# A transformer block on one Trainium2 core: the shift's part of two bias sums as one-column TensorE products, and shorter chains of one-column operations

## The chip, the cores and the metric

The kernel runs on one core of a Trainium2 chip. The core has five engines that run at the same time, each through its own queue in order: TensorE multiplies (PE, and PEld for its weight loads), VectorE (DVE), ScalarE (ACT) and GpSimd (POOL) work elementwise, and SyncE (SP) issues the loads from memory. They wait for each other by semaphores. The metric is device time in microseconds. Before the change three runs took 2125.7, 2130.1 and 2131.35 us.

## The reference, cut to what matters

One layer on 512 positions of 2048 channels. A conditioning vector c gives six modulation vectors through w_ada; the first two, shift1 and scale1, modulate the normalized input, and one large projection w_in makes Fourier channels, queries, keys, values, gates and output gates of it.

```
mod = jax.nn.silu(c) @ w_ada + b_ada
shift1, scale1, gate1, shift2, scale2, gate2 = jnp.split(mod, N_MOD, axis=-1)
h = modulate(rms_norm(x, norm1_w), shift1, scale1)      # h * (1 + scale) + shift
p = h @ w_in
q_in, k_in, v_in = p[..., o1:o2], p[..., o2:o3], p[..., o3:o4]
```

Behind it come the Fourier mixer and four mLSTM heads, the output projection, and a gated feed-forward network with a depthwise convolution.

## The kernel before, in words

Channels lie on the 128 partitions, in 16 tiles (k = 0 to 15) of 128 channels x 512 positions. Every float32 operand of a product is split into a rounded high half and a low half (`split`, lines L120 on ScalarE and L121 on VectorE; tiles named wg0h, wg0l and so on), and a product is three: high by high, high by low, low by high (lines L235 to L237 in `kouter`).

The modulation vectors are made on VectorE: `ada_unit` loads 128 x 1024 numbers of w_ada (tile ad, names like ad0_7_0 for modulation 0, k = 7, half 0) and multiplies them by silu(c) with a sum along the row (L167), two units for each k. `ada_cols` then adds the two partial sums, the bias (and 1 for a scale) and, for a scale, multiplies by the norm's weight: two or three operations on a single column (L183, L186, L189). Eight ad buffers take turns.

The first stage ("o-gate", sums g0 to g7) runs over k with x times scale1's column A1, before shift and norm are known. While it runs, the sum of squares is collected.

The second stage (sums h0 to h5: queries and keys of three heads, 768 columns of weights a step, tiles wh0 to wh15, four raw buffers and three each of high and low halves) still multiplies the unshifted x. Meanwhile the shift's columns S1 are made, and `shift_tile` rebuilds every tile of the input as x times A1 times rb1 (the reciprocal root as a row, L456) plus S1: ht on VectorE (L433, L435, L436), then the high half mov on ScalarE (L439) and the low half on VectorE (L440). What shift contributes to the h sums has to be added as a bias for each output column. For the first head's query and key (256 columns) this is done from the raw weight tiles that are in memory anyway: qkb, a 128 x 256 tile, collects weight times S1 over k on VectorE (L442, L444), and at the end two products with a column of ones sum it over the partitions (L465). For all other columns the weights are read a second time (`bias_units`, tiles wb, accumulated into sb on VectorE). GpSimd multiplies the eight o tiles by rb1 once that is there. After the second stage come the first head's values with the gates (`natural_gates`, tiles v_0 to v_5), the fourth head's queries (q), and the heads.

All instructions are put in order by the framework, which plans each engine's queue from a simulated timeline of its own; only what is wrapped in `pinned` keeps the order of the source.

Of the kernel before, what the change touches and what calls it, by code (L numbers as in the profile page):

```python
# [10 lines left out]
F32 = mybir.dt.float32  # L11
# [3 lines left out]
ALU = mybir.AluOpType  # L15
PSUM = bass.MemoryType.PSUM

P = 128
D = 2048
S = 512  # L20
KT = D // P
# [30 lines left out]
def block_kernel(ctx: ExitStack, tc: tile.TileContext, xT, vec, wada, wg, wqk, wv0, wvu,  # L52
                 wout, wup, wdown, cst, rmask, ftab, crow, cvec, outT):
    nc = tc.nc
    mm = nc.tensor.matmul
# [17 lines left out]
    def T512(name, dt=F32):  # L73
        return tmp["p"].tile([P, S], dt, tag="t", name=name)
# [6 lines left out]
    def load_consts():  # L81
        nc.sync.dma_start(vt, vec)
        nc.scalar.activation(vcols("c", 0, KT), vcols("c", 0, KT), AF.Silu)
        ident0 = T512("ident0")
        nc.sync.dma_start(ident0[:, 0:P], cst[:, 0:P])
        nc.vector.tensor_copy(identr, ident0[:, 0:P])

    onesf = const.tile([P, P], F32, name="onesf")
# [14 lines left out]
    def vcols(n, i, w):  # L103
        return vt[:, VC[n] + i:VC[n] + i + w]

    def raw_tile(src, w, name):
        r = wp.tile([P, 1024], F32, tag="raw", bufs=4, name=name)
        nc.sync.dma_start(r[:, :w], src)
        return r
# [3 lines left out]
    def split(src, w, name, into=None):  # L113
        if into is None:
            hi = wp.tile([P, 1024], F32R, tag="whi", name=name + "h")
            lo = wp.tile([P, 1024], F32R, tag="wlo", name=name + "l")
        else:
            hi, lo = into[:, 0:1024], into[:, 1024:2048]
        put = tc.keep_in_program_order if inorder[0] else lambda i: i
        put(nc.scalar.activation(hi[:, :w], src, AF.Copy))  # L120
        put(nc.vector.tensor_tensor(lo[:, :w], src, hi[:, :w].bitcast(F32), op=ALU.subtract))  # L121
        return hi, lo
# [14 lines left out]
    def bcast_rows(ps, cols, put):  # L137

        dg = T512("dg")
        for j in range(cols.shape[1]):  # L140
            sl = slice(j * P, (j + 1) * P)
            nc.vector.tensor_scalar(dg[:, sl], ident, cols[:, j:j + 1], None, op0=ALU.mult)
            put(ps[:, sl], onesf, dg[:, sl], start=True, stop=True)
# [3 lines left out]
    adaD = const.tile([P, 2, KT, 4], F32, name="adaD")  # L147
# [10 lines left out]
    def ada_unit(mod, slot, k, u, w, sb, pool=None):  # L158

        if "ring" in ada:  # L160
            r = ada["ring"][k % 4]
        else:
            r = ada["p"].tile([P, w], F32, tag="ar", bufs=ada["n"], name=f"ad{mod}_{k}_{u}")
        nc.sync.dma_start(r, wada[mod, k, :, u * w:(u + 1) * w])
        part = adaD[:, slot, k, u:u + 1]
        if not ((k if w == S else u) % 2 if pool is None else pool):
            nc.vector.scalar_tensor_tensor(r, r, 1.0, sb, op0=ALU.mult, op1=ALU.mult, accum_out=part)  # L167
        else:
            ada["pool"] = nc.gpsimd.tensor_tensor(r, r, sb, op=ALU.mult)
            ada["late"].append((r, part))  # L170
            if w == S:
                ada_late(1 if "ring" in ada else 2)

    def ada_late(n):
        while len(ada["late"]) > n:
            r, part = ada["late"].pop(0)
            nc.scalar.activation(r, r, AF.Copy, accum_out=part)

    def ada_cols(dst, kind, mod, slot, k0, n, parts):

        ada_late(0)
        s = slice(k0, k0 + n)
        nc.vector.tensor_tensor(dst, adaD[:, slot, s, 0], adaD[:, slot, s, 1], op=ALU.add)  # L183
        for i in range(2, parts):
            nc.vector.tensor_tensor(dst, dst, adaD[:, slot, s, i], op=ALU.add)
        nc.vector.scalar_tensor_tensor(dst, dst, 0.0 if kind == "g" else 1.0, vcols("bada", mod * 16 + k0, n),  # L186
                                       op0=ALU.add, op1=ALU.add)
        if kind != "g":
            nc.vector.tensor_tensor(dst, dst, vcols(kind, k0, n), op=ALU.mult)  # L189
# [4 lines left out]
    def big_tiles(k):  # L194
        return mov512[:, k, :], mov512[:, KT + k, :]
# [4 lines left out]
    def side(name):  # L200
        return pss.tile([P, S], F32, tag="s", name=name)
# [3 lines left out]
    pst = pa.enter_context(ExitStack())  # L205
    pS = pst.enter_context(tc.tile_pool(name="pS", bufs=1))
    silb = pS.tile([P, D], F32, tag="silb", name="silb")
    ada.update(p=pS, n=8)
    o_t = [None] * 8

# [136 lines left out]
    def pinned(f, *a, **kw):  # L347
        return tc.keep_in_program_order(f(*a, **kw))
# [4 lines left out]
    def load_x(k):  # L353
        x = (pS if 8 <= k < 13 else pX).tile([P, S], F32, tag=f"x{k}", name=f"x{k}")
        pinned(nc.sync.dma_start, x, xT[k])
        x_t.append(x)
# [3 lines left out]
    def scale_tile(k):  # L360
        ak = A1[:, k:k + 1]
        for u in (range(2) if k else (1, 0)):
            ada_unit(1, 0, k, u, 1024, silb[:, u * 1024:(u + 1) * 1024], pool=False)
        if k == 0:
            load_x(0)
            load_consts()
        r = raw_tile(wg[k, :, 0:1024], 1024, f"wg{k}")
        if k + 1 < KT:
            load_x(k + 1)
        ada_cols(ak, "n1", 1, 0, k, 1, 2)  # L370
        t = x_t[k]
        bt[k], btl[k] = big_tiles(k)
        nc.scalar.activation(bt[k], t, AF.Copy, scale=ak)
        nc.vector.scalar_tensor_tensor(btl[k], t, ak, bt[k].bitcast(F32), op0=ALU.mult, op1=ALU.subtract)
        w = split(r, 1024, f"wg{k}")
        if k == 0:
            nc.scalar.activation(ssq1, t, AF.Square)
        else:
            sq = T512("sq")
            nc.scalar.activation(sq, t, AF.Square)  # L380
            nc.vector.tensor_tensor(ssq1, ssq1, sq, op=ALU.add)
        return w
# [9 lines left out]
    for k in range(KT):  # L392
        nxt = scale_tile(k + 1) if k + 1 < KT else None
        kouter(g_ps, *w, k)
        w = nxt
# [3 lines left out]
    def rstd_cols(ssqs, t, put=mm):  # L399

        cp = side("ssc")
        n = (t.stop - t.start) // P
        for j in range(n):
            for i, q in enumerate(ssqs):
                put(cp[:, j:j + 1], q[:, t.start + j * P:t.start + (j + 1) * P], onesf[:, 0:1], start=i == 0,
                    stop=i == len(ssqs) - 1)
        rc = tiny.tile([P, 4], F32, tag="rc", name="rc")[:, 0:n]
        rsqrt_cols(rc, cp[:, 0:n], n, 1.0 / D)
        return rc

    def row_rstd(rc, put=mm):

        rps = side("rps")
        bcast_rows(rps, rc, put)
        return rps[:, 0:rc.shape[1] * P]
# [11 lines left out]
    def shift_tile(k, r):  # L427

        sk = S1[:, k:k + 1]
        t = T512("ht")  # L430
        raw = 0 < k < 13
        if raw:
            nc.vector.scalar_tensor_tensor(t, x_t[k], A1[:, k:k + 1], rb1, op0=ALU.mult, op1=ALU.mult)  # L433
        else:
            nc.vector.tensor_tensor(t, bt[k].bitcast(F32), btl[k].bitcast(F32), op=ALU.add)  # L435
            nc.vector.tensor_tensor(t, t, rb1, op=ALU.mult)  # L436
        ada_cols(sk, "g", 0, 0, k, 1, 2)
        bt[k], btl[k] = big_tiles(k)
        nc.scalar.activation(bt[k], t, AF.Identity, bias=sk)  # L439
        nc.vector.scalar_tensor_tensor(btl[k], t, sk, bt[k].bitcast(F32), op0=ALU.add, op1=ALU.subtract)  # L440
        if k == 0:
            nc.vector.tensor_scalar(qkb, r[:, 0:256], sk, None, op0=ALU.mult)  # L442
        else:
            nc.vector.scalar_tensor_tensor(qkb, r[:, 0:256], sk, qkb, op0=ALU.mult, op1=ALU.add)  # L444

    w = g2_weights(0)
    rb1 = pX.tile([P, S], F32, tag="x0", name="rb1")
    rc1 = rstd_cols([ssq1], slice(0, S))
    qkb = pS.tile([P, 256], F32, tag="qkb", name="qkb")
    bias = const.tile([P, 14], F32, name="bias")  # L450
    done = []
    for k in range(KT):
        nxt = g2_weights(k + 1) if k + 1 < KT else None
        kouter(g_ps, *w[1], k)
        if k == 0:
            nc.vector.tensor_copy(rb1, row_rstd(rc1, partial(pinned, mm)))  # L456
        if k:
            shift_tile(*done.pop())
        shift_unit(k)
        done.append((k, w[0]))  # L460
        w = nxt
    shift_tile(*done.pop())
    cp = side("qkbp")
    for i in range(2):
        mm(cp[:, i:i + 1], qkb[:, i * P:(i + 1) * P], onesf[:, 0:1], start=True, stop=True)  # L465
    nc.vector.tensor_copy(bias[:, 8:10], cp[:, 0:2])
    raws = []
    for i, x in enumerate((7, 6, 2, 3, 4, 5)):
        r = pX.tile([P, S], F32, tag=f"x{x}", name=f"qkraw{i}")
# [217 lines left out]
    for h in range(NH):  # L687
# [9 lines left out]
        for i in range(2):  # L697
            j = 2 * h + i
            if j < 6:
                r = raws[j]  # L700
                nc.vector.tensor_scalar(r, r, bias[:, 8 + j:9 + j], None, op0=ALU.add)
            else:
                r = q3 if j == 6 else proj(1, "k3")
# [146 lines left out]
    for m in range(LAST[0]):  # L850
        if m < 4:
            ps = first[m][0]
        else:
            ps, g = wo_tile(m)
# [508 lines left out]
    for it, t in enumerate(TAIL):  # L1363
        n = t.stop - t.start
# [120 lines left out]
```

## Time and profile before

| | |
|---|---|
| median of three runs | 2130.1 us |
| profiled execution, its span | 2123.46 us, 2121.7 us |
| busy: TensorE, VectorE, ScalarE, GpSimd | 95%, 83%, 48%, 10% of the span |
| chain that ended last | TensorE 66%, DMA 15%, VectorE 13% |

The shares are averages over stages with different limits: the 16 accumulations (L442, L444) and the products L465 belong to the second stage alone, from 95 to 191 us of the span. How a stage runs is read from its own stretch: which engine never idles there, and what ends the idle time of the one that does. Engines work on instructions one behind another that overlap by a few hundredths of a microsecond, so the price of one is the distance from its start to the next start.

### The profile page before, as it was taken

The page shows a single profiled execution, that of the slowest core. Times are in us where ns is not written, and L with a number is a line of the kernel's source. Part 1 is how long each engine was busy: PE and PEld are TensorE (multiplying, and loading weights), DVE is VectorE, ACT ScalarE, POOL GpSimd, SP SyncE. Part 2 cuts the span into 40 slices and gives each one's busy share as a digit, 9 for nine tenths or more (in the row PEclk, how much of TensorE's full clock was granted, in tenths as well). Part 3 has the DMA queues.
Part 4 walks back from the last instruction along what each step waited for, and adds up shares of the span by engine and source line. Part 5 has one row for each costly group of instructions (what it writes and reads, how often), then busy time and mean ns, then how long its engine had stood idle before and what let it go on. Part 6 is the DMA issues. An engine that isn't in the chain of part 4 may idle for free.

```text
span 2121.7 us, 38452 instructions
## 1 busy us (share of the span) xinstructions
PE 2017.6 (95%) x15036; PEld 1931.7 (91%) x15036; DVE 1769.0 (83%) x2888; ACT 1020.3 (48%) x1469; POOL 221.6 (10%) x255
## 2 busy tenths in 40 slices
PE   8988998999899799999999999999999899999996
PEld 6877997998789699999999999999999899999996
DVE  8999978787777889899899999889888677777756
ACT  4422353443224655555555555555555455555553
POOL 0020000000000010101101101101100111111134
PEclk9999998999999899999999999999999999999998
DMA  9965846473887375676577577656667797887684
GB/s 373 367 232 189 288 140 199 159 247 130 302 282 260 85 215 157 194 216 191 162 222 222 156 211 213 183 179 200 196 161 292 244 288 212 246 246 196 161 237 153
DMA packets 165434, 456.41 MB, mean 215 GB/s; under 512 B 18354, under 2 KB 22978, under 8 KB 165252
## 3 DMA queue, kind: packets, MB, share of 16 engines
q1 hardware_dynamic: 135860, 371.64, 51.3%
q0 software_dynamic: 28304, 81.28, 17.9%
q8 instruction: 117, 1.92, 0.4%
q10 hardware_dynamic: 1088, 1.05, 0.1%
q14 instruction: 65, 0.53, 0.1%
HBM read 386.52 MB, written 67.37 MB: 214 GB/s over the span
## 4 chain that ended last, share of the span: by engine, by line
PE 66%; DMA 15%; DVE 13%; issue 3%; ACT 2%; POOL 1%; SPq 0%; POOLq 0%; DVEq 0%; ACTq 0%
DMA ad<-wada 4%; DVE ad L167 3%; DMA ring<-wada 2%; DMA gkept<-gh 2%; PE un L320 1%; PE un L318 1%; PE un L319 1%; PE g L235 1%; PE g L236 1%; PE g L237 1%; PE N L622 1%; PE wo L283 1%; PE wo L284 1%; PE wo L282 1%; PE vn L318 1%
## 5 line engine op out<-in xcount | busy, mean ns | idle before, releaser
L167 DVE SCALAR_TENSOR_TENSOR ad<-ad,silu 128x512 f32<-128x512 f32 x185 | 122.2, 686 | 17.8 <-DMA ad<-wada 17.4
L1326 POOL DMA_DIRECT2D xkept<-cr x80 | 68.8, 981 | 382.6 <-DVE cr L1131 364.3
L1193 ACT ACTIVATE u<-cr,cvt 128x512 f32<-128x512 f32 x88 | 71.6, 815 | 28.8 <-DVE cr L1129 27.3
L167 DVE SCALAR_TENSOR_TENSOR ad<-ad,silb 128x1024 f32<-128x1024 f32 x64 | 78.7, 1235 | 7.8 <-DMA ad<-wada 7.7
L1195 DVE SCALAR_TENSOR_TENSOR u<-cr,cvt,u 128x511 f32<-128x511 f32 x88 | 65.4, 745 | 0.5 <-ACT u L1193 0.5
L1196 DVE SCALAR_TENSOR_TENSOR u<-cr,cvt,u 128x511 f32<-128x511 f32 x88 | 65.5, 744 | 0.0
L167 DVE SCALAR_TENSOR_TENSOR ring<-ring,silu 128x512 f32<-128x512 f32 x71 | 47.2, 688 | 17.1 <-DMA ring<-wada 16.8
L1242 POOL DMA_DIRECT2D gkept<-gh x38 | 29.6, 779 | 235.9 <-ACT gh L1237 193.3
L1240 DVE TENSOR_TENSOR gst<-gst,gh 128x1024 fp32r<-128x1024 f32 (+1 forms) x38 | 41.4, 1089 | 11.6 <-ACT gh L1237 11.4
L1237 ACT ACTIVATE gh<-gst 128x1024 fp32r<-128x1024 f32 (+1 forms) x38 | 36.0, 947 | 29.0 <-DMA gkept<-gh 25.4
L1011 POOL DMA_DIRECT2D xkept<-xc x6 | 4.1, 681 | 422.1 <-DVE A L189 408.5
L283 PE MATMUL dz<-mov,dz_0h 128*128 128x256 f32 (+1 forms) x156 | 48.1, 309 | 0.0
L282 PE MATMUL dz<-mov,dz_0h 128*128 128x256 f32 (+1 forms) x156 | 47.9, 307 | 0.0
L284 PE MATMUL dz<-mov,dz_0l 128*128 128x256 f32 (+1 forms) x156 | 47.9, 308 | 0.0
L284 PE MATMUL wo<-mov,wo_8l 128*128 128x512 f32 x104 | 41.4, 398 | 3.6 <-DVE wo_8l L121 3.6
L282 PE MATMUL wo<-mov,wo_8h 128*128 128x512 f32 x104 | 40.8, 399 | 1.5 <-ACT mov L793 1.5
L283 PE MATMUL wo<-mov,wo_8h 128*128 128x512 f32 x104 | 41.3, 398 | 0.8 <-DVE mov L794 0.7
L284 PE MATMUL wo<-mov,wo_0l 128*128 128x512 f32 x104 | 40.7, 391 | 0.8 <-DVE wo_0l L121 0.8
L282 PE MATMUL wo<-mov,wo_0h 128*128 128x512 f32 x104 | 40.6, 391 | 0.0
L283 PE MATMUL wo<-mov,wo_0h 128*128 128x512 f32 x104 | 40.6, 390 | 0.0
L622 PE MATMUL N<-v,ph 128*128 128x258 f32 x160 | 35.0, 298 | 3.3 <-ACT hn L633 2.9
L120 ACT ACTIVATE dz_0h<-dz 128x768 fp32r<-128x768 f32 x26 | 22.0, 845 | 30.4 <-PE dz L283 23.6
(4032 smaller groups left out, 9411.0 us busy)
## 6 DMA issues: line engine op xcount, KB each, us to landing
ad<-wada SPq DMA_DIRECT2D x185, 256.0 KB, 4.6
ad<-wada SPq DMA_DIRECT2D x64, 512.0 KB, 8.6
mov<-gkept SPq DMA_DIRECT2D x52, 512.0 KB, 10.2
xkept<-cr POOLq DMA_DIRECT2D x80, 256.0 KB, 6.0
ring<-wada SPq DMA_DIRECT2D x71, 256.0 KB, 5.0
wo<-wout SPq DMA_DIRECT2D x32, 512.0 KB, 4.9
wb<-wg SPq DMA_DIRECT2D x48, 256.0 KB, 5.0
dz<-wdown SPq DMA_DIRECT2D x26, 384.0 KB, 3.5
```

The lines of the kernel that those rows point to most:

```text
L167: nc.vector.scalar_tensor_tensor(r, r, 1.0, sb, op0=ALU.mult, op1=ALU.mult, accum_out=part)
L282: mm(ps, wh[:, sl], rh[k], start=st, stop=False)
L283: mm(ps, wh[:, sl], rl[k], start=False, stop=False)
L284: mm(ps, wl[:, sl], rh[k], start=False, stop=sp)
L318: mm(acc[t], bt[k][:, sl], wh[:, sw], start=False, stop=False)
L622: mm(np_[:, 0:258], l[:, sl], v[:, r, t, :], start=i == 0, stop=i == n - 1)
L1193: nc.scalar.activation(u, r, AF.Identity, bias=cv(3, ch), scale=cv(1, ch))
L1195: nc.vector.scalar_tensor_tensor(u[:, 1:S], r[:, 0:S - 1], cv(0, ch), u[:, 1:S], op0=ALU.mult, op1=ALU.add)
L1196: nc.vector.scalar_tensor_tensor(u[:, 0:S - 1], r[:, 1:S], cv(2, ch), u[:, 0:S - 1], op0=ALU.mult, op1=ALU.add)
L1237: nc.scalar.activation(hi, part, AF.Copy)
L1240: nc.vector.tensor_tensor(lo, part, hi.bitcast(F32), op=ALU.subtract)
L1326: nc.gpsimd.dma_start(xkept[4 * d + 2 * j + r], rows[j][r], accum_op=ALU.add)
```

## The change

Two edits. In `ada_cols`, a single column with two partial sums is now made by one operation that adds both sums and the bias (a scale's bias plus 1 is made once for all 16 columns, b1p), followed for a scale by the multiplication with the norm's weight. And qkb is no longer a tile of VectorE: for each k two float32 TensorE products, with 128 raw weight columns as the stationary side and the column S1 as the moving side, add up in two PSUM columns qkb0 and qkb1, which are copied into the bias at the end.

```diff
     def ada_cols(dst, kind, mod, slot, k0, n, parts):
         ada_late(0)
+        if n == 1 and parts == 2:
+            col = [adaD[:, slot, k0, i:i + 1] for i in range(2)]
+            b = vcols("bada", mod * 16 + k0, 1) if kind == "g" else b1p[:, k0:k0 + 1]
+            nc.vector.scalar_tensor_tensor(dst, col[0], col[1], b, op0=ALU.add, op1=ALU.add)
+            if kind != "g":
+                nc.vector.tensor_tensor(dst, dst, vcols(kind, k0, n), op=ALU.mult)
+            return
...
+        if k == 0:
+            nc.vector.tensor_scalar(b1p, vcols("bada", 16, KT), 1.0, None, op0=ALU.add)
         ada_cols(ak, "n1", 1, 0, k, 1, 2)
...
-        if k == 0:
-            nc.vector.tensor_scalar(qkb, r[:, 0:256], sk, None, op0=ALU.mult)
-        else:
-            nc.vector.scalar_tensor_tensor(qkb, r[:, 0:256], sk, qkb, op0=ALU.mult, op1=ALU.add)
+        for i in range(2):
+            mm(qkb[i], r[:, i * P:(i + 1) * P], sk, start=k == 0, stop=k == KT - 1)
...
-    qkb = pS.tile([P, 256], F32, tag="qkb", name="qkb")
+    qkb = []
...
             nc.vector.tensor_copy(rb1, row_rstd(rc1, partial(pinned, mm)))
+            qkb += [side(f"qkb{i}")[:, 0:1] for i in range(2)]
...
-    cp = side("qkbp")
     for i in range(2):
-        mm(cp[:, i:i + 1], qkb[:, i * P:(i + 1) * P], onesf[:, 0:1], start=True, stop=True)
-    nc.vector.tensor_copy(bias[:, 8:10], cp[:, 0:2])
+        nc.vector.tensor_copy(bias[:, 8 + i:9 + i], qkb[i])
```

The planner orders the engines anew. TensorE in the second stage, where the products of the fourth weight tile (wh3) end: before, wh4 follows at once (h0 and h1 are sums, wh4h the high half).

```order
L237 MATMUL h5_881<-mov_76,wh3l_993 128x512
L235 MATMUL h0_876<-mov_76,wh4h_1029 128x512
L236 MATMUL h0_876<-mov_76,wh4h_1029 128x512
L235 MATMUL h1_877<-mov_76,wh4h_1029 128x512
L236 MATMUL h1_877<-mov_76,wh4h_1029 128x512
```

Now, at the same place (S1 is the shift's column, wh0 to wh4 without a letter the raw tiles):

```order
L245 MATMUL h5_867<-mov_76,wh3l_980 128x512
L452 MATMUL qkb0_931<-S1_84,wh2_939 128x1
L452 MATMUL qkb0_931<-S1_84,wh3_977 128x1
L452 MATMUL qkb1_932<-S1_84,wh0_868 128x1
L452 MATMUL qkb1_932<-S1_84,wh1_896 128x1
L452 MATMUL qkb1_932<-S1_84,wh2_939 128x1
L452 MATMUL qkb1_932<-S1_84,wh3_977 128x1
L452 MATMUL qkb0_931<-S1_84,wh4_1014 128x1
L452 MATMUL qkb1_932<-S1_84,wh4_1014 128x1
L243 MATMUL h0_862<-mov_76,wh4h_1016 128x512
```

The row broadcast of the reciprocal root and two more qkb products stand just ahead of these rows; before, that broadcast stood among the products of wh5. In the new order the qkb products of k = 5 to 7 stand between wh4h and wh4l, and those of k = 8 to 13 each behind the products of the next tile (k + 1).

ScalarE at the same time, from the high half of wh3 on. Before:

```order
L120 ACTIVATE wh3h_992<-wh3_990 128x768
L120 ACTIVATE wh4h_1029<-wh4_1027 128x768
L120 ACTIVATE wh5h_1066<-wh5_1064 128x768
L120 ACTIVATE wh6h_1103<-wh6_1101 128x768
L120 ACTIVATE wh7h_1140<-wh7_1138 128x768
L439 ACTIVATE mov_76<-ht_976,S1_84 128x512
```

Now:

```order
L120 ACTIVATE wh3h_979<-wh3_977 128x768
L449 ACTIVATE mov_76<-ht_963,S1_84 128x512
L449 ACTIVATE mov_76<-ht_1001,S1_84 128x512
L449 ACTIVATE mov_76<-ht_1038,S1_84 128x512
L449 ACTIVATE mov_76<-ht_1075,S1_84 128x512
L120 ACTIVATE wh4h_1016<-wh4_1014 128x768
L120 ACTIVATE wh5h_1053<-wh5_1051 128x768
```

Four high halves of shifted input tiles stand ahead of wh4h now. Also on ScalarE, earlier, wh1h stands behind the third copy of an o sum instead of ahead of the first.

VectorE around the low half wh4l. Before (rs_y, rs_z and rc belong to the reciprocal root, ad0_6_0 is the unit of k = 6):

```order
L167 SCALAR_TENSOR_TENSOR ad0_5_1_1135,adaD_89<-ad0_5_1_1135,silb_99 128x1024
L186 SCALAR_TENSOR_TENSOR S1_84<-S1_84,vt_77 128x1
L133 SCALAR_TENSOR_TENSOR rs_z_897<-rs_y_896 128x4
L183 TENSOR_TENSOR S1_84<-adaD_89 128x1
L444 SCALAR_TENSOR_TENSOR qkb_909<-wh4_1027,S1_84,qkb_909 128x256
L121 TENSOR_TENSOR wh4l_1030<-wh4_1027,wh4h_1029 128x768
L134 TENSOR_TENSOR rs_z_897<-rs_z_897,rs_v_895 128x4
L186 SCALAR_TENSOR_TENSOR S1_84<-S1_84,vt_77 128x1
L167 SCALAR_TENSOR_TENSOR ad0_6_0_1169,adaD_89<-ad0_6_0_1169,silb_99 128x1024
```

Now:

```order
L167 SCALAR_TENSOR_TENSOR ad0_10_1_1307,adaD_89<-ad0_10_1_1307,silb_99 128x1024
L443 SCALAR_TENSOR_TENSOR ht_1186<-x6_337,A1_83,rb1_874 128x512
L443 SCALAR_TENSOR_TENSOR ht_1223<-x7_382,A1_83,rb1_874 128x512
L167 SCALAR_TENSOR_TENSOR ad0_11_0_1341,adaD_89<-ad0_11_0_1341,silb_99 128x1024
L443 SCALAR_TENSOR_TENSOR ht_1260<-x8_427,A1_83,rb1_874 128x512
L443 SCALAR_TENSOR_TENSOR ht_1297<-x9_472,A1_83,rb1_874 128x512
L121 TENSOR_TENSOR wh4l_1017<-wh4_1014,wh4h_1016 128x768
L121 TENSOR_TENSOR wh5l_1054<-wh5_1051,wh5h_1053 128x768
```

The low half of wh4 stood between the ad units of k = 5 and k = 6; now it stands behind that of k = 11 and behind the ht of k = 9. On SyncE the load of wh4 moved from behind ad0_5_1 to behind ad0_11_0, followed there by those of wh5 to wh7, and the first twelve loads of the bias sums (wb) now stand among those of wh12 to wh15, ahead of the first value tiles.

## Rows read from the trace of the kernel before

**Rows 1.** Stretches (start:end us, length, busy us per engine, granted clock, DMA).
```profile
14.00:95.00 81.00, 81.00 (x348) 66.79 (x348) 80.02 (x158) 33.53 (x46) 0.00 (x0) 1.00 1.02 395
141.00:175.00 34.00, 20.39 (x73) 15.63 (x74) 34.00 (x63) 7.34 (x10) 0.34 (x1) 0.86 0.38 120
191.00:217.00 26.00, 24.91 (x197) 24.67 (x197) 22.85 (x41) 8.88 (x12) 0.00 (x0) 1.00 0.96 342
217.00:336.00 119.00, 119.00 (x878) 112.86 (x877) 100.55 (x233) 49.85 (x82) 2.15 (x1) 1.00 0.63 213
336.00:376.00 40.00, 31.24 (x207) 29.59 (x206) 32.30 (x113) 12.66 (x29) 0.00 (x0) 0.83 0.50 170
516.00:556.00 40.00, 32.61 (x160) 26.32 (x159) 34.98 (x96) 12.78 (x21) 0.00 (x0) 0.96 0.78 262
```

**Rows 2.** Timeline of PE, 104 to 192 us (start us, us, instruction, idle before).
```profile
104.39 0.94 PE L405 MATMUL ssc<-onesf,ssq 128*128 128x1 f32 x8
...
116.44 0.39 PE L235 MATMUL h<-mov,wh3h 128*128 128x512 f32 x1
...
120.52 0.39 PE L235 MATMUL h<-mov,wh4h 128*128 128x512 f32 x1
...
145.90 2.93 PE L237 MATMUL h<-mov,wh8l 128*128 128x512 f32 x6 [5.26 <-DVE wh8l L121]
...
152.04 0.42 PE L235 MATMUL h<-mov,wh9h 128*128 128x512 f32 x1
...
191.12 0.38 PE L341 MATMUL v<-v_0h,mov 128*128 128x272 f32 x1
```

**Rows 3.** Timeline of DVE, 98 to 162 us.
```profile
98.71 0.96 DVE L121 TENSOR_TENSOR wh1l<-wh,wh1h 128x768 fp32r<-128x768 f32 x1 [1.31 <-ACT wh1h L120]
...
105.37 0.16 DVE L130 TENSOR_SCALAR rs_v<-ssc 128x4 f32<-128x4 f32 x1 [2.03 <-PE ssc L405]
...
115.94 0.95 DVE L121 TENSOR_TENSOR wh4l<-wh,wh4h 128x768 fp32r<-128x768 f32 x1
...
126.41 0.68 DVE L456 COPY rb<-rps 128x512 f32<-128x512 f32 x1
...
155.73 1.22 DVE L167 SCALAR_TENSOR_TENSOR ad<-ad,silb 128x1024 f32<-128x1024 f32 x1
...
156.88 2.07 DVE L433 SCALAR_TENSOR_TENSOR ht<-x,A,rb 128x512 f32<-128x512 f32 x3
158.87 0.95 DVE L121 TENSOR_TENSOR wh10l<-wh,wh10h 128x768 fp32r<-128x768 f32 x1
...
161.54 0.48 DVE L444 SCALAR_TENSOR_TENSOR qkb<-wh,S,qkb 128x256 f32<-128x256 f32 x1
161.94 0.15 DVE L183 TENSOR_TENSOR S<-adaD 128x1 f32<-128x1 f32 x1
```

**Rows 4.** Timeline of ACT, 97 to 134 us.
```profile
97.83 0.85 ACT L120 ACTIVATE wh1h<-wh 128x768 fp32r<-128x768 f32 x1 [4.37 <-issue]
100.28 4.03 ACT L213 ACTIVATE o<-g 128x512 f32<-128x512 f32 x8 [1.60 <-PE g L237]
...
133.42 0.72 ACT L439 ACTIVATE mov<-ht,S 128x512 fp32r<-128x512 f32 x1 [8.00 <-DVE ht L436]
```

**Rows 5.** DMA issues, 0 to 240 us (KB each, median us to landing).
```profile
wh<-wg SPq DMA_DIRECT2D x16, 384.0 KB, 5.4
```

**Rows 6.** Timeline of DVE while GpSimd works, 127 to 142 us.
```profile
127.94 1.52 DVE L444 SCALAR_TENSOR_TENSOR qkb<-wh,S,qkb 128x256 f32<-128x256 f32 x1
129.38 2.31 DVE L167 SCALAR_TENSOR_TENSOR ad<-ad,silb 128x1024 f32<-128x1024 f32 x1
...
133.31 8.58 DVE L433 SCALAR_TENSOR_TENSOR ht<-x,A,rb 128x512 f32<-128x512 f32 x5
```

**Rows 7.** Timeline of POOL, 126 to 142 us.
```profile
127.24 14.09 POOL L348 TENSOR_TENSOR o<-o,rb 128x512 f32<-128x512 f32 x8 [126.80 <-DVE S L183]
```

**Rows 8.** Chain that ended last, 0 to 240 us (start us, us, work).
```profile
216.64 0.47 PE q L282
```

More of the change, by code (lines that the diff above doesn't have):

```diff
@@ L207, in block_kernel @@
     silb = pS.tile([P, D], F32, tag="silb", name="silb")
+    b1p = pS.tile([P, KT], F32, tag="b1p", name="b1p")
     ada.update(p=pS, n=8)
```

## The prediction

> **What bounds the kernel now.** I read the stretches first. From 14 to 95 us (the o-gate stage) TensorE never stops, 81.00 of 81.00 us, and VectorE is busy for 80.02. From 141 to 175, in the second stage (queries and keys of three heads, its sums called h), TensorE works for only 20.39 of 34 us, its granted clock averages 0.86, and VectorE is busy for all 34.00: there VectorE is the bound [rows 1]. TensorE's own rows name the place and the price. It stood 5.26 us for wh8l, the low half of the ninth weight tile, which VectorE writes; then six products took 2.93 us, and only at 152.04 were starts 0.23 apart again. The 14 products from 145.90 to 152.04 took 6.1 us where 14 of 0.227 (18 from 116.44 to 120.52) take 3.2: the stop cost another 3 us at the lower clock of 1.2 GHz [rows 2]. Last I read the order of the instructions of both kernels, since the change alters it on every engine up to the first tiles of the output projection and leaves it alone behind.
>
> **What goes and what comes.** VectorE loses 16 accumulations qkb at 0.40 us (start at 161.54, the next operation at 161.94 [rows 3]), 6.4 us, and 32 operations on one column at 0.07 to 0.15, some 3.5 us; it gains one 16-column operation and one more copy, 0.3 us. In the o-gate stage the saved columns buy nothing, as TensorE is the bound there. TensorE gains 32 one-column float32 products and loses two. The same form stands in the trace as ssc: four products of two passes each, 0.94 us, so 0.23 each and about 7 us in all [rows 2]. Where TensorE waits anyway they cost nothing. The two new PSUM tiles take the two side buffers that h4 and h5 leave; nothing else wants one before the stage ends.
>
> **What the order makes of it.** I walk the new order with the durations of the rows.
>
> *To 122 us.* In the o-gate stage nothing moves for TensorE, so h starts at 103.25 as before (five products ahead of ssc, 104.39 [rows 2]). ScalarE now has wh1h behind the third o copy instead of ahead of the first. The copies start at 100.28 and take 0.50 each, wh1h 0.85: done at 102.6 [rows 4]. VectorE stands at wh1l until then; before it went on at 98.71. With wh1l 0.9 (158.87) and two ad products of 1.15 (155.73 to 156.88) it begins the reciprocal root rs_v at 105.8, before at 105.37 [rows 3]: the wait has eaten what three accumulations and the columns saved. From rs_v to the copy rb1 it took 21.0 us before (126.41); of that two ad, three low halves, three accumulations and some columns, 6.4 us, no longer stand in front, which makes 120.4. TensorE gets there at about the same time: 71 products of 0.227, ssc and the row broadcast at some 0.85 each, 121.0 in all. rb1 is there at 121.7, some 5 us earlier than before.
>
> *The first new stop.* On TensorE eight qkb products follow (1.9 us, to about 123), and then those of wh4, ahead of wh4h. Two things hold them. The load of wh4 stood in SyncE's queue behind ad0_5_1; now it is behind ad0_11_0, which needs the buffer of ad0_7_0 (eight buffers, two a step), free at 120.9, and it also waits for the qkb product of k=0, at 122.1, because the raw tile is held until TensorE has read it. With 5.4 us to land [rows 5] it is there at 127.8. That is not the last: on ScalarE wh4h now stands behind four activations mov, and each of these waits for a tile ht of VectorE. In that stretch GpSimd multiplies the eight o tiles by rb1, and a VectorE operation then takes about 1.05 us more: qkb 1.52, ad 2.31, five ht 8.58 [rows 6], while GpSimd has its 14.09 us [rows 7]. From 121.7: ad 2.24, ht 1.7 and three ht 5.1 give 130.8, the fourth mov 0.7 [rows 4], wh4h 0.85: 132.3. TensorE stands from 123 to 132.3.
>
> At this place a rule bears on the sum. In these rows every VectorE operation with two tensors in SBUF pays the extra, and eight of them stand beside eight GpSimd operations. The Trainium skill ("SBUF — State Buffer", its terms, "shared port pair") says that the two engines lock one pair of ports for a whole instruction and the loser blocks; the trace agrees. By the price of the one slow accumulation its removal would give 1.44 us; by the rule the 14 us stay, another operation takes the place, and it gives 0.40. The walk above has the 14 us in either case.
>
> *The second.* TensorE does twelve wh4h products at the low clock (0.43 each, to 137.5) and the six qkb of wh5 to wh7, and then needs wh4l. VectorE had that at 115.94 [rows 3]; now it is behind the ht of k=9. From ad0_8_0, done at 136.4: six ad 6.9, eight operations on 512 columns at 0.66 (three from 156.88 to 158.87) 5.3, two columns 0.1, wh4l 0.9 [rows 3]: 149.6. TensorE stands from 139 to 149.6.
>
> *To the end of the stage.* From there TensorE has 204 products, 46.3 us, 3.0 for the low clock after the stop, and 20 qkb, 4.7: 203.6. The feed holds by my walk: wh7l at 158 against 162 needed, wh8l at 163 against 167; wh12 to wh15 load after the qkb product four tiles back and are split 1 to 3 us ahead of need. Before, the first product of the value stage started at 191.12 [rows 2]. So the stage ends 12.5 us later: 19.9 us of stops instead of 13.6, and 6 us of new products on the path.
>
> *Behind it.* The values took 24.91 busy of 26 us [rows 1] and VectorE has the same steps before q, so q starts about 12 us later than 216.64 [rows 8]. But the first loads of the bias sums no longer wait for the stage's last product: twelve are issued inside the stage, and nine more accumulations of 0.66 are done before q, 6 us of VectorE. TensorE cannot use that before 336, being busy for 119.00 of 119.00 from 217; from 336 to 376 it idles for 8.8 us at a clock of 0.83, from 516 to 556 for 7.4 [rows 1]. I let 3.5 come back, between none and 6. Sum: +12.5 − 3.5 = +9. The profiled execution took 2123.5 (span 2121.7); with +9 it is 2132.5. The median of the three runs lies 6.6 above it; I carry the difference: **2139 us**. Its own range: the walk may be off by 3 each way, and nothing or all 6 may come back: +3.5 to +15.5, 2134 to 2146.
>
> **Rivals.** *The relief reaches TensorE (faster).* TensorE stands 13.6 us for VectorE in 141 to 175 [rows 1], and VectorE has 9.6 us less to do. If all of it comes off those stops, and 10 of the 32 products lie outside them (2.3), the kernel gains 7.3: 2122.8. It turns on whether VectorE reaches wh4l before TensorE is through with wh4h; where it does, the second stop is gone. For it speaks the VectorE-bound stretch, against it the order, which puts wh4l behind a dozen long operations more. The far end would be all 13.6 us of stops and 3 of low clock gone, less 7 of products: −10.
>
> *The delay is absorbed (the same).* The idle 8.8 and 7.4 us after 336 are TensorE waiting while VectorE works through ad products. Their loads do not need h. If they keep their time, TensorE comes 12 later and finds them done: 9 or more come back, +3, 2133. Against it: in the new order these products still follow the bias sums in one queue.
>
> *The late loads miss (slower still).* wh13, wh14 and wh15 now stand behind bias loads in SyncE's queue, which wait for VectorE. My margins are 1 to 3 us; if three miss by 2 and the clock falls once (3), it is 9 more: 2148.
>
> **Chances.** The forecast 0.46, late loads 0.11, absorbed 0.26, faster 0.17. About 0.3%, 6.4 us, is what a measurement of this kernel can tell from no change. The forecast's lower edge lies inside that, the upper cases of the absorbed one outside, which nearly cancels: slower 0.56, the same 0.27, faster 0.17. The range leaves a tenth at either end, below the faster case and above late loads: 2122 to 2149.
>
> **What would show it.** Right: TensorE's waits name a qkb product or wh4h by ScalarE near 123 (9 us) and wh4l by VectorE near 139 (10 us); wh1l waits 4 us longer on VectorE; rb1 near 121; the stops for wh8l to wh12l are gone; the value stage starts near 203. Wrong: TensorE fed through wh4 and wh5, the value stage before 195, or a q that starts 12 late with the delay gone by 560.

## The result, and the profile after

The changed kernel takes 2142.4 us (median of 5 executions, 2139.6 to 2148.1) against 2130.1 (5 executions, the three above among them, 2123.1 to 2131.4): the ratio over all executions is 1.0072, 95% interval 1.0051 to 1.0092. It is slower by 12.3 us by the medians and by some 15 us by the ratio. The prediction was 2139 and slower. The profiled execution took 2139.63 us (span 2137.5, mean granted clock 0.977); that of before 2123.46 (2121.7, 0.983).

The stretches of the changed kernel, with the columns of [rows 1]. The first, fourth, sixth and last two answer to rows there; the other three lie ahead of the new stops, on the first of them, and behind.

```profile
14.00:95.00 81.00, 81.00 (x353) 66.93 (x352) 80.43 (x145) 34.14 (x45) 0.00 (x0) 1.00 1.03 403
95.00:120.00 25.00, 25.00 (x120) 20.98 (x119) 19.12 (x49) 6.32 (x11) 0.00 (x0) 1.00 0.67 226
120.00:141.00 21.00, 10.12 (x47) 8.70 (x45) 20.90 (x22) 5.09 (x7) 14.39 (x8) 0.64 0.65 230
141.00:175.00 34.00, 26.30 (x108) 21.65 (x109) 33.14 (x62) 8.25 (x11) 0.00 (x0) 0.82 0.50 164
175.00:203.00 28.00, 28.00 (x144) 23.75 (x144) 17.56 (x27) 8.95 (x12) 0.00 (x0) 1.00 0.54 176
203.00:229.00 26.00, 22.52 (x179) 22.29 (x177) 21.18 (x34) 6.89 (x10) 0.00 (x0) 0.99 0.89 301
348.00:388.00 40.00, 36.82 (x288) 35.56 (x288) 33.52 (x107) 13.54 (x30) 0.00 (x0) 1.00 0.57 183
528.00:568.00 40.00, 31.57 (x148) 25.53 (x147) 35.05 (x94) 11.13 (x18) 0.00 (x0) 0.91 0.85 295
```

VectorE had slack from 95 to 120 (19.12 of 25) and again from 175 on (17.56 of 28). In between it was full, and TensorE worked for 10.12 of 21 us at a clock of 0.64, and at 0.82 in the next stretch. So the relief did arrive on VectorE, but beside the stretch in which TensorE waits for it.

TensorE's timeline there, against [rows 2]:

```profile
102.81 0.95 PE L415 MATMUL ssc<-onesf,ssq 128*128 128x1 f32 x8
...
127.48 1.02 PE L452 MATMUL qkb<-S,wh 128*128 128x1 f32 x4 [5.37 <-DMA wh<-wg]
...
130.34 0.80 PE L243 MATMUL h<-mov,wh4h 128*128 128x512 f32 x1 [1.85 <-ACT wh4h L120]
...
148.70 2.93 PE L245 MATMUL h<-mov,wh4l 128*128 128x512 f32 x6 [11.37 <-DVE wh4l L121]
...
200.27 0.95 PE L452 MATMUL qkb<-S,wh 128*128 128x1 f32 x8
201.08 0.38 PE L349 MATMUL v<-v_0h,mov 128*128 128x272 f32 x1
```

Two stops stand in place of those for wh8l to wh12l: 5.4 and 1.9 us for wh4's load and its high half, then 11.4 us for its low half. The value stage starts at 201.08 instead of 191.12, 10.0 later. VectorE, against [rows 3, 6]:

```profile
101.50 0.96 DVE L121 TENSOR_TENSOR wh1l<-wh,wh1h 128x768 fp32r<-128x768 f32 x1 [5.77 <-ACT wh1h L120]
...
104.67 0.16 DVE L130 TENSOR_SCALAR rs_v<-ssc 128x4 f32<-128x4 f32 x1
...
120.22 0.69 DVE L464 COPY rb<-rps 128x512 f32<-128x512 f32 x1
...
121.97 1.75 DVE L446 TENSOR_TENSOR ht<-ht,rb 128x512 f32<-128x512 f32 x1
123.64 8.46 DVE L443 SCALAR_TENSOR_TENSOR ht<-x,A,rb 128x512 f32<-128x512 f32 x5
132.03 2.29 DVE L167 SCALAR_TENSOR_TENSOR ad<-ad,silb 128x1024 f32<-128x1024 f32 x1
...
134.25 1.22 DVE L185 SCALAR_TENSOR_TENSOR S<-adaD,vt 128x1 f32<-128x1 f32 x1
...
147.70 0.94 DVE L121 TENSOR_TENSOR wh4l<-wh,wh4h 128x768 fp32r<-128x768 f32 x1
```

rb1 is ready 6 us earlier than before. wh4l, which stood at 115.94, comes at 147.70, behind the ht and mov of the shift. ScalarE and SyncE's queue against [rows 4, 5], and GpSimd against [rows 7]:

```profile
100.61 0.86 ACT L120 ACTIVATE wh1h<-wh 128x768 fp32r<-128x768 f32 x1
...
128.83 0.72 ACT L449 ACTIVATE mov<-ht,S 128x512 fp32r<-128x512 f32 x1 [0.96 <-DVE ht L443]
129.46 0.83 ACT L120 ACTIVATE wh4h<-wh 128x768 fp32r<-128x768 f32 x1
```

```profile
121.50 2.02 SPq L108 DMA_DIRECT2D wh<-wg  x4
```

```profile
121.07 14.39 POOL L356 TENSOR_TENSOR o<-o,rb 128x512 f32<-128x512 f32 x8 [120.62 <-DVE rb L464]
```

Four loads of weight tiles leave right behind one another from 121.50, when the first products qkb have read the raw tiles.

Behind the value stage q starts at 230.6 instead of 216.64 [rows 8], 14.0 later, not 10. TensorE's wait there, and the accumulations sb of the bias sums on VectorE ahead of it:

```profile
PE q L290 <- DVE v L234: 5.1, 1, 5.1
```

```profile
173.95 0.49 DVE L505 TENSOR_SCALAR sb<-wb,S 128x512 f32<-128x512 f32 x1 [0.86 <-DMA wb<-wg]
...
185.75 0.75 DVE L510 SCALAR_TENSOR_TENSOR sb<-wb,S,sb 128x512 f32<-128x512 f32 x1
...
207.98 0.49 DVE L505 TENSOR_SCALAR sb<-wb,S 128x512 f32<-128x512 f32 x1
...
226.72 1.42 DVE L510 SCALAR_TENSOR_TENSOR sb<-wb,S,sb 128x512 f32<-128x512 f32 x2 [1.20 <-DMA wb<-wg]
228.06 0.17 DVE L672 COPY gt<-v 128x16 f32<-128x16 f32 x1
...
230.02 0.42 DVE L234 TENSOR_TENSOR v<-v,v 128x256 fp32r<-128x256 f32 x1
```

The copies gt and the splits of v stand behind 24 accumulations sb, each of which needs a load of its own; before, behind 14. Six of the 24 ran inside the second stage (173.95 to 186), the other 18 from 207.98 on in the value stage, where the 14 stood before. By the first product of the feed-forward part the delay is 6.8 us in this profile, and 9.8 in a second one (below).

### The profile page after: what moved, and what is told of

Its sections match the earlier page's. It is cut to its first block, busy times and chain, and to the rows that moved or that the text cites. A ratio compares the mean times of both kernels' runs of the same rounds, so it can differ in the third digit from the quotient of the medians.

```text
span 2137.5 us, 38499 instructions
## 1 busy us (share of the span) xinstructions
PE 2026.8 (95%) x15096; PEld 1943.9 (91%) x15096; DVE 1761.7 (82%) x2842; ACT 1018.3 (48%) x1469; POOL 220.5 (10%) x255
## 4 chain that ended last, share of the span: by engine, by line
PE 69%; DMA 13%; DVE 12%; issue 3%; ACT 2%; POOL 1%; SPq 0%; POOLq 0%; DVEq 0%; ACTq 0%
DMA ad<-wada 3%; DVE ad L167 2%; DMA ring<-wada 2%; DMA gkept<-gh 2%; PE un L326 1%; PE un L328 1%; PE un L327 1%; PE g L243 1%; PE g L244 1%; PE g L245 1%; PE N L629 1%; PE vn L328 1%; PE vn L327 1%; PE vn L326 1%; PE wo L292 1%
## 5 line engine op out<-in xcount | busy, mean ns | idle before, releaser
L1247 DVE TENSOR_TENSOR gst<-gst,gh 128x1024 fp32r<-128x1024 f32 (+1 forms) x38 | 41.4, 1089 | 12.4 <-ACT gh L1244 12.4
L510 DVE SCALAR_TENSOR_TENSOR sb<-wb,S,sb 128x512 f32<-128x512 f32 x44 | 31.5, 744 | 5.8 <-DMA wb<-wg 5.7
```

Source lines behind the costliest of these rows:

```text
L1247: nc.vector.tensor_tensor(lo, part, hi.bitcast(F32), op=ALU.subtract)
```

## The experiments

All of them ran beside the kernel before. The table gives what the later points use: how much later than in before's first profile the value stage (v), q, and the feed-forward's first product (up) start, the length of the stretch from that product to the last product of the down stage, and the ratio of the times with its interval. The starts were read to 0.1 us, so a difference can be 0.1 off.

| kernel | v | q | up | stretch, us | ratio |
|---|---|---|---|---|---|
| before (first profile) | 191.1 | 216.6 | 690.7 | 1410.5 | |
| before2 | +0.2 | −0.4 | +0.7 | 1422.1 | 1.0013 (0.9999–1.0027) |
| after (first profile) | +10.0 | +14.0 | +6.8 | 1418.9 | 1.0072 (1.0051–1.0092) |
| after2 | +10.0 | +14.6 | +9.8 | 1419.3 | 1.0070 (1.0056–1.0084) |
| cols | +2.6 | +4.1 | +0.4 | 1421.7 | 1.0007 (0.9991–1.0023) |
| qkb | +12.4 | +18.1 | +10.2 | 1420.8 | 1.0051 (1.0034–1.0068) |
| none | −6.3 | −3.9 | −5.6 | 1419.0 | 0.9968 (0.9954–0.9983) |
| hold | +7.5 | +10.5 | +8.5 | 1412.0 | 1.0035 (1.0022–1.0049) |
| half | +6.7 | +6.9 | +0.3 | 1414.9 | 1.0003 (0.9990–1.0016) |
| inord | +6.3 | +7.1 | −0.1 | 1418.5 | 1.0000 (0.9986–1.0015) |
| late | −2.9 | −0.9 | −1.9 | 1422.4 | 0.9989 (0.9970–1.0009) |
| late2 | −2.6 | −0.7 | −3.3 | 1425.1 | 0.9994 (0.9979–1.0008) |
| pool | −3.3 | −1.3 | −4.0 | 1416.5 | 0.9979 (0.9963–0.9996) |
| poolin | −4.9 | −0.3 | −2.5 | 1426.8 | 0.9998 (0.9981–1.0016) |

**cols: the fused columns alone.** The kernel before with the new branch of `ada_cols` and `b1p`; the sums stay as they were.

> The kernel before with the fused column operations alone; the sums stay on VectorE. Theory A (the one-column products hold the raw tiles and two PSUM banks, the order built around that hold puts the splits of wh4 to wh7 behind the shift work, and TensorE stops twice): the order of these splits stays that of before, no 11 us stop for wh4l; 2127 to 2132 us, ratio to before 0.999 to 1.001. Rival B (the fused columns, by the shorter VectorE chain, moved the splits): the 11 us stop for wh4l is here too, and 2137 to 2143 us.

No difference in time that can be told. TensorE's two longest waits from 95 to 240 us are those of before (4.8 and 5.3 us there), for low halves of later tiles; none is for wh4l:

```profile
PE h L245 <- DVE wh12l L121: 5.5, 1, 5.5
PE h L245 <- DVE wh8l L121: 4.6, 1, 4.6
```

Rival B falls: the fused columns do not bring the stop for wh4l, and the 2.6 us at v and 4.1 at q by which this kernel is later are gone by up (0.4).

**qkb: the products alone.** The changed kernel without the branch and `b1p`.

> The kernel before with the sums as one-column products alone; the columns are computed as before. Theory A (hold and order): both stops of TensorE, for wh4h near 130 us and for wh4l near 148 us, 2138 to 2146 us, ratio 1.004 to 1.008. Rival B (the fused columns moved the splits): wh4l waits under 3 us, 2130 to 2135 us, the price of the 32 products being about 4.7 us.

2139.4 us. Both stops are here, and the wait at q; the last row is one more wait:

```profile
PE h L237 <- DVE wh4l L121: 10.8, 1, 10.8
PE q L282 <- DVE v L226: 6.8, 1, 6.8
PE qkb L442 <- DMA wh<-wg: 6.1, 1, 6.1
PE qkb L442 <- DVE rb L454: 1.1, 1, 1.1
```

So the loss belongs to the sums' part of the change. The last row names what the products wait for at their start: the copy rb1. Of the four side tiles in PSUM, h4 and h5 hold two, and the row broadcast holds one until rb1 is copied from it; so the products of the second column, and with them the raw tiles, wait for rb1.

**none: neither products nor accumulations.**

```diff
-        for i in range(2):
-            mm(qkb[i], r[:, i * P:(i + 1) * P], sk, start=k == 0, stop=k == KT - 1)
...
-        nc.vector.tensor_copy(bias[:, 8 + i:9 + i], qkb[i])
+    nc.vector.memset(bias[:, 8:10], 0.0)
```

> The changed kernel without the first head's shift sums (the two bias columns are set to zero; nothing else is left out): VectorE is relieved of the sixteen operations and TensorE has no product in their place. Theory A (hold and order): the splits of wh4 to wh6 stand ahead of the four mov again, no stop over 4 us for a split between 120 and 150 us, the value stage begins near 184 to 188 us (7 to 3 us ahead of before), 2118 to 2126 us. Rival C (the products' own time on TensorE is the loss): the time is that of the changed kernel less 5 us, 2136 to 2139 us. Rival D (the relief of VectorE is worth nothing): 2129 to 2132 us.

2122.3 us, 6.8 below before by the ratio: the relief of VectorE is worth that much. The loads of wh3 to wh7 leave one at a time as the splits free their tiles, the first and last of five being

```profile
102.31 0.33 SPq L108 DMA_DIRECT2D wh<-wg  x1
...
118.01 0.33 SPq L108 DMA_DIRECT2D wh<-wg  x1
```

wh4l is split early, and no stop of TensorE between 120 and 150 us is over 2.6 us:

```profile
113.87 0.95 DVE L121 TENSOR_TENSOR wh4l<-wh,wh4h 128x768 fp32r<-128x768 f32 x1
```

```profile
133.20 1.65 PE L245 MATMUL h<-mov,wh6l 128*128 128x512 f32 x6 [2.07 <-DVE wh6l L121]
140.18 1.66 PE L245 MATMUL h<-mov,wh7l 128*128 128x512 f32 x6 [2.60 <-DVE wh7l L121]
```

Rivals C (2136 to 2139) and D (2129 to 2132) both fall.

**hold: the hold without the products.** To `none` one ScalarE operation on one column is added in `shift_tile`:

```diff
+        hold = tiny.tile([P, 1], F32, tag="hold", name="hold")
+        nc.scalar.activation(hold, r[:, 0:1], AF.Identity, bias=bt[k][:, 0:1].bitcast(F32))
```

> The kernel without the sums (they are left out, two bias columns zero), with one more ScalarE operation of one column per block that reads the raw tile and the shifted tile, and so holds each raw tile until its shift is in; no product is added on TensorE. The order of the splits then is that of the changed kernel. Theory A (the hold and the order that follows from it): the stops of the changed kernel come back, wh4l's at 9 to 13 us, though TensorE has no product more; the value stage at 194 to 198 us against 184.8 without the hold; 2127 to 2135 us. Rival C (the products on TensorE make the loss): as the kernel without the sums, 2119 to 2125 us.

2134.9 us. TensorE has nothing more to do than in `none`, and the stops are back, 24.1 us in all instead of 18.6 in the changed kernel:

```profile
131.11 0.79 PE L243 MATMUL h<-mov,wh4h 128*128 128x512 f32 x1 [10.29 <-ACT wh4h L120]
...
150.37 2.08 PE L245 MATMUL h<-mov,wh4l 128*128 128x512 f32 x4 [13.78 <-DVE wh4l L121]
```

with the four loads together again (the queue, then VectorE):

```profile
126.82 4.15 SPq L108 DMA_DIRECT2D wh<-wg  x4
```

```profile
149.38 0.94 DVE L121 TENSOR_TENSOR wh4l<-wh,wh4h 128x768 fp32r<-128x768 f32 x1
```

This settles what makes the stops. The stop for wh4l (13.8 us) and the start of v (198.6) lie just beyond what theory A expected, the time inside it. Holding the raw tile until the shift is in, and the order of splits that follows, costs 0.67% of the time against `none`, some 14 us, and 13.8 us at v, without one product on TensorE.

**half: one product per tile.** The loop over `i` in `shift_tile` runs once, and there is one PSUM column instead of two; the key sums are left out.

> The changed kernel with one of the two products of each tile (the key sums' product is left out, and the query sums stand in both bias columns): half of the products' work on TensorE, the same hold of the raw tiles and of a PSUM bank behind rb1, and the same order of the splits. Theory A (hold and order): both stops as in the changed kernel, wh4l's at 10 to 12 us; the changed kernel less the half of 5 us: 2138 to 2142 us. Rival C (the products' own time, or what it does to TensorE, is the loss): half of the distance to the kernel without the sums comes back, 2130 to 2134 us.

2130.5 us: theory A missed by 8 to 12 us, and the number is rival C's. The stops are there all the same:

```profile
127.71 0.58 PE L452 MATMUL qkb<-S,wh 128*128 128x1 f32 x2 [5.44 <-DMA wh<-wg]
131.40 0.79 PE L243 MATMUL h<-mov,wh4h 128*128 128x512 f32 x1 [3.10 <-ACT wh4h L120]
147.29 2.93 PE L245 MATMUL h<-mov,wh4l 128*128 128x512 f32 x6 [10.32 <-DVE wh4l L121]
```

At v it is 3.3 us ahead of the changed kernel: the second stop ends 1.4 us earlier (147.29 instead of 148.70), and eight products fewer behind it are the other 1.9. The next 4 come at q: here 16 accumulations sb of the value stage stand ahead of the first copy gt instead of 18, and q waits 1.3 us instead of 5.1. So up to q this is the products' price and the order once more, not a new cost of a product. Up to the feed-forward part the distance is 6.5 us, 9.5 from the second profile; the times are 12 (medians) to 15 (ratios) apart. The rest is not settled. Nor do the stops alone make the loss over before: `half` has 18.9 us of them, as many as the changed kernel, and the time of before. It makes up 6.6 us between q and up, where `hold`, 0.8 us later at v, makes up 2.0; what decides that no run shows.

**inord: products and hold as they are, the splits' order fixed.** `inorder[0] = True` from the stage's first split to its last, so that `split` keeps the order of the program on ScalarE and VectorE.

> The changed kernel with the splits of the second stage held in the order of the program on ScalarE and VectorE: wh3l and wh4l then stand between the shift work instead of behind it, and wh4h behind three mov instead of four. The hold of the raw tiles stays. Theory A in the form that the order of the splits on VectorE is most of the loss: the stop of 11 us for wh4l falls under 5 us, others of 1 to 3 us stay, 2128 to 2136 us. Theory A in the form that the hold of the raw tiles alone sets it (wh4 lands late whatever the order): 2139 to 2146 us.

2131.2 us, the time of before: with the splits' order fixed the whole loss is gone, and the hold is still there. The stop for wh4l is gone. Two are left, 12.6 us instead of 18.6, now for wh3, and longer than the 1 to 3 us expected:

```profile
126.54 0.80 PE L243 MATMUL h<-mov,wh3h 128*128 128x512 f32 x1 [5.63 <-ACT wh3h L120]
...
139.58 2.92 PE L245 MATMUL h<-mov,wh3l 128*128 128x512 f32 x6 [6.94 <-DVE wh3l L121]
```

v is 3.7 us ahead of the changed kernel, and q 6.9, with a wait of 1.8 us there; the rest of the 15 us comes back behind q, as in `half`.

**late and late2: products without a hold.** They stand behind the loop and read the 256 columns from loads of their own. In `late` these loads fetch columns 0 to 255, not those that the sums are over; `late2` fetches the right ones.

```diff
+    for j in range(4):
+        q = pS.tile([P, 1024], F32, tag="ar", bufs=8, name=f"qw{j}")
+        nc.sync.dma_start(q.rearrange("p (k c) -> p k c", k=4),
+                          wg[4 * j:4 * j + 4, :, 1024:1280].rearrange("k p c -> p k c"))
...
+            mm(cp[:, i:i + 1], qw[k // 4][:, o:o + P], S1[:, k:k + 1], start=k == 0, stop=k == KT - 1)
```

> The changed kernel with the 32 products moved behind the loop: they read the 256 columns from four loads of their own (2 MB more DMA) into tiles that the shift's modulation blocks leave, so no raw tile is held for them; columns fused. Theory A (hold and order): no stop over 4 us between 120 and 150 us; the time of the kernel without the sums plus 32 products at two passes of 0.09 us, 5 us or less: 2121 to 2131 us. Rival C (the products' own time on TensorE is the loss): as the changed kernel, 2138 to 2144 us. Rival E (the extra 2 MB of loads delay the weights of the stage that follows): the value stage starts with a wait on a load, 2132 to 2140 us.

> As the kernel with the products behind the loop, but its four loads read the columns 1024 to 1279 of the weights that the sums are over (the one before read columns 0 to 255, the same amount). The same order, so the same time: 2124 to 2133 us, ratio to before 0.997 to 1.001. If where the columns lie in memory mattered, it would differ from it by over 5 us.

2129.4 and 2126.2 us; the two agree. No stop in the second stage is over 2.6 us. The 64 passes of `late2` on TensorE:

```profile
171.91 1.39 PE L478 MATMUL qkbp<-S,qw 128*128 128x1 f32 x12
177.33 1.62 PE L478 MATMUL qkbp<-S,qw 128*128 128x1 f32 x14
184.38 4.30 PE L478 MATMUL qkbp<-S,qw 128*128 128x1 f32 x38
```

They are 7.3 us of busy time, and v comes 3.8 us later than in `none`. About half of it does not show there, because `none` waits 4.4 us ahead of v for VectorE (qkraw, the h sums times rb1), and the run of 38 stands in that place. The times are 4 to 6 us above `none` by the ratios, which uses up what the relief brings. Neither rival C nor rival E is seen.

**pool: the sums on ScalarE and GpSimd.**

```diff
+        d = r[:, 0:256] if k else qkb
+        nc.scalar.activation(d, r[:, 0:256], AF.Copy, scale=sk)
+        if k:
+            nc.gpsimd.tensor_tensor(qkb, qkb, d, op=ALU.add)
```

> The sums neither on VectorE nor on TensorE: ScalarE scales the 256 columns of each raw tile by the shift's column (in place, behind the split), GpSimd adds them up; the column is computed right behind its modulation block; columns fused. GpSimd's products with rb1 move behind these sums. Theory A (the loss is the hold and the order, the relief of VectorE is worth about 7 us): the order of the splits is nearly that of the kernel without the sums, no stop over 5 us, 2120 to 2127 us. Rival F (GpSimd's additions slow VectorE's operations with two inputs beside them, or the scaling delays the splits on ScalarE): 2129 to 2138 us.

2123.2 us, 4.5 below before by the ratio and 0.9% below the changed kernel: the fastest version that computes everything, though the gain over before is small beside what can be told. GpSimd's additions take 1.28 us on average (19.2 for 15, 0.77 to 2.02 each) and the longest stop for a split is 4.3 us:

```profile
151.92 0.79 PE L245 MATMUL h<-mov,wh9l 128*128 128x512 f32 x1 [4.30 <-DVE wh9l L121]
```

**poolin: the same with the splits in the order of the program.**

> The kernel with the sums on ScalarE and GpSimd, with the splits of the second stage in the order of the program besides. If the waits of 1 to 4 us for splits that it still has are the order's doing, 2116 to 2122 us; if they are VectorE's load, 2121 to 2127 us; if the fixed order makes ScalarE and VectorE wait at the head (wh0 behind the scaling), 2128 to 2136 us.

2126.0 us, ratio 0.9998: no gain on `pool`, nor a clear loss. v is 1.6 us earlier, but q waits 5.7 us. The waits for splits stay (2.8, 3.9 and 2.6 us are the longest), so the order does not make them, and TensorE waits only 0.9 us for wh0 at the head. The time lies in the range for VectorE's load, but that this load makes the waits is not shown apart. The fixed order helped where it took the place of a bad one.

**after2 and before2: both kernels again.**

> The changed kernel unaltered, with more executions. If the part of its loss that appears in the feed-forward stage of its profile (7 us over before's profile, with the same instructions in the same order) is the scatter of single executions: 2136 to 2142 us and a ratio to before of 1.004 to 1.006. If it is the change's: ratio 1.006 to 1.008.

> The kernel before unaltered, with another profile. If before's first profile was a short one of a scatter: the stretch from the first product of the feed-forward's first block to the last product of the down stage takes 1414 to 1425 us here, as in the other kernels, against 1410.5 in the first; the time 2126 to 2133 us, ratio 1.000. If it is a property of this kernel: 1409 to 1412 us again.

The changed kernel takes 2142.7 us (2140.3 to 2145.2), and the ratio of 1.0070 is in the range of the second reading: with more executions the loss does not shrink. Before's second profile has the same v, q and up within 0.7 us, and a stretch behind of 1422.1 us against 1410.5: it varies by 12 us between two executions of one kernel, and the changed kernel's 1418.9 and 1419.3 lie between. So the 8 us by which the first profiles differ there can't be put down to the change, and profiles alone can't show a part of the loss that lies there.

## Why the prediction was right, point by point

*The relief.* The rival sum put it at 7.3 us with some products on the path; `none` measures 6.8 with none of them. Of the 9.6 us that it took off VectorE, the 3.5 for the columns were too many: two operations of 0.07 us (161.94 to 162.01, 163.15 to 163.22) gave way to one of 0.13 (142.63 to 142.76), so in the second stage the accumulations are nearly all of it. In the changed kernel the relief did not reach TensorE, because of the point on which that rival turned: VectorE came to wh4l at 147.70, long after TensorE had begun wh4h at 130.34.

*To 122 us.* "Nothing moves for TensorE" in the o-gate stage was off by about one: h began at 102.13 instead of 103.25, and ssc, behind three products of h instead of five, came at 102.81. wh1h was done at 101.5 (102.6 predicted), VectorE waited 4.5 us longer there (4), rs_v stood at 104.7 (105.8) and rb1 was ready at 120.9 (121.7).

*The first stop.* It came from where the walk had it: the load of wh4, behind the buffer and the read of the raw tile, landed at 127.5 (127.8). wh4h was done at 130.3, not 132.3: GpSimd began at 121.07, so the first ad, at 120.83, did not pay the extra that the walk gave it, and ScalarE's path was shorter by 1.1 us; 0.8 more is the earlier rb1. The two parts are 7.2 us against 9.3.

*The port.* The slow accumulation is gone, and GpSimd's row still shows 14.39 us. ht 1.75, five ht 8.46 and ad 2.29 pay as before, and the eighth is a column operation S of 1.22 us, whose like takes 0.13 (142.63 to 142.76) when GpSimd is idle. The Trainium skill ("SBUF — State Buffer", terms, "shared port pair") has the loser blocked for a whole instruction; the trace agrees, and the removal brought only the accumulation's own 0.4 us: the eight took 13.9 us before (127.94 to 141.81) and take 13.4 now (121.97 to 135.39).

*The second stop.* 11.4 us to 148.70, predicted 10.6 to 149.6; `hold` and `inord` show that the order, which follows from the hold, is its cause.

*To the end of the stage.* 201.1 against 203.6: 0.9 from the second stop's end, 0.8 from the products, and 0.8 from the low clock, which held eleven products 0.43 apart, to 153.46, and cost 2.2 instead of 3.0. The products were miscounted: of 32, eight, two and six stand ahead of wh4l, so 16 are left, not 20. They cost 3.9 us instead of 4.7, 0.25 each for the twelve between other products (172.75 to 177.34 is 4.59 us, and the 18 products of a tile alone take 4.08) and 0.20 for the last four. Those 0.20 could be read from ssc as well, from its start to the next start (104.39 to 105.19); the 0.23 is from start to end. TensorE was fed throughout (28.00 of 28 us from 175), so the late loads did not miss.

*Behind it: the term that was mis-sized.* The twelve loads of the bias sums did leave inside the stage (170.7 to 186.5), and ten more accumulations started before q (26 instead of 16; nine were forecast). But only six of them ran inside the stage, and "the same steps before q" did not hold: in the value stage 18 stood ahead of the first gt instead of 14. What was to give time back cost 4 us first: q was 14 late, not 12, though the stage had ended 2.5 us earlier than forecast. Then more came back than in the walk: 7.2 us up to the feed-forward part in the first profile and 4.8 in the second, so the delay there is 6.8 and 9.8 against +9. In the stretch of the absorbed rival TensorE idles 3.2 us instead of 8.8, at a clock of 1.00 instead of 0.83 [rows 1], so part of what that rival forecast came; that ad products done early are the reason is not shown.

*The total.* The forecast was 9 us above the median, the measurement is 12 to 15. Up to the feed-forward part the profiles account for 7 to 10. The other 5 or so are less than the scatter of the stretch behind between two profiles; the repeated ratio says that they are there, and what makes them stays open. That +9 lies between 6.8 and 9.8 is in part luck: the walk made the second stage 2.5 us too long, the value stage 4 too short, and gave 1 to 4 too little back, and these cancel. By the ratios the parts are −0.32% for the relief (`none`), +0.67% for the hold and its order (`hold`), and 0.36%, 7.7 us, for the 32 products (the changed kernel against `hold`), which at 0.20 to 0.25 each are 6 to 8 us. `half` does not fit this sum: it would be at 1.0053 and measures 1.0003.

## What to carry to other kernels

An engine's load is not the only price of an operation: ask how long it holds its inputs. Moving a cheap accumulation to an engine that reaches it later held four weight tiles and reordered the splits, and in `hold` this cost, without any product, twice what the relief was worth. Where a scheduler sets the order, compare the position of the next stage's first producer in both orders before counting busy time.

## What was not expected of the hardware

A VectorE operation on one column, 0.13 us from start to start, took 1.14 beside GpSimd's tensor operations (134.25 to the next start at 135.39): the extra of 1.0 us is that of operations on 256 to 1024 columns (1.0 to 1.1), so it does not depend on the size here. A one-column float32 product costs 0.20 us back to back (eight passes in 0.81), 0.25 between other products, and 0.11 per pass in the run of 38. And two executions of one kernel differed by 11.6 us in one stretch in which every engine has the same instructions, so a single pair of profiles can't show a change of that size there.
